# Evacuations of the output projection queued first, combinations in eight pieces, and a lead of four groups

## The chip, the cores and the metric

The kernel runs on one core of one Trainium2 chip. The metric is the device time of one execution in microseconds; less is better. The core's engines each work through a queue of their own in order: PE (matrix products), DVE (elementwise on vectors), ACT (elementwise with functions, and copies), POOL (elementwise), SP (which issues all the DMAs here). Semaphores order them between each other.

## The reference

An encoder trunk of four residual layers on 1024 tokens of width 1024, all in float32: attention (two head groups) with an output projection, an MLP, a gated unit with an output projection, another MLP, and a last norm. The part that the change touches is what follows an output projection:

```python
def _mlp(x, norm_g, w1, w2):
    h = _rmsnorm(x, norm_g)
    return x + jnp.square(jax.nn.relu(h @ w1)) @ w2
# after   x + concatenate([oa, ob]) @ w_out      (attention layer)
# and     x + y @ w_out                          (gated unit)
```

`w1` is 1024 by 4096, `w2` 4096 by 1024. The norm's factor per token is applied behind `h @ w1`, so that the products can start from `x * norm_g` before the sum of squares is known.

## The kernel before

Activations lie transposed: `x[k][:, half]` holds 128 of the 1024 features (k = 0 to 7) for 512 of the tokens (half 0 or 1). Every float32 operand of a product is split into a high half, a copy in fp32r made by ACT, and a low half, the rest, made by DVE (`hilo`, L144 to L148, `scaled`, L833); a product of two operands is three matmuls (`mm3`).

The output projection, `out_proj` (L828), goes in two column groups cg and two halves of tokens through `lin` (L272). At the end of each half four accumulators are complete, and `ev` (L869) evacuates them: DVE adds the accumulator to `x` (L872), ACT squares the sum and POOL adds the square into a running sum `ss` (L313, L314), SP stores the sum, and `combine` (L839) prepares the operands of the MLP. The MLP's first product is done with seven products of half size in place of eight (a scheme of Strassen's kind): the blocks of `x` by k < 4 or k >= 4 and half 0 or 1 are combined into seven operands `hc[i, kk]`, i = 1 to 7, kk = 0 to 3. Operands 1 and 2 are blocks alone (half 0, known early); 5 is a difference of blocks with k < 4; 7, 6, 4 and 3 need the last half of the last column group. For each of its four k, `combine` makes b22 on ACT (L850), t3 and t2 on DVE (L851, L853), and the halves of operands 7 and 6 from them; a function `rest` (L856) makes operands 4 and 3 later. The four `rest` are collected in `later`.

In `mlp` (L885) the products of the 16 groups of columns of `w1` go in the order of a table, `UP_ORDER` (L153): first i = 1 for the first `LEAD` = 3 groups, then i = 2 for these, then 7, 6, 5, 4, 3 of group 0, of group 1, of group 2, and then all seven of each further group. Product (g, i) here means group g, operand i: 12 matmuls. i = 1 fills a bank of PSUM, which ACT copies out (r1, L916); i = 2 adds onto the same bank, so it waits for that copy. i = 3 adds onto the bank of i = 5, after DVE has read it (L936). After the product (0, 7) the two `ssb` matmuls sum the squares over the features, and L321 or L324 on ACT and L325 to L331 on DVE make the norm's factor. PSUM has eight such banks, given out in turn as they come free. At each step `ahead` (L131, called at L966) makes the weights for four steps ahead (DVE adds, ACT and DVE split), and at step 1 all four `rest` run (L968 to L970).

The framework's scheduler puts the instructions of each engine into an order at build time; it is not quite the order of the text. The two passages from an output projection into an MLP are the same code, called at L881 and L1243.

Of the kernel before, what the change touches and what calls it, by code (L numbers as in the profile page):

```python
# [7 lines left out]
F32 = mybir.dt.float32  # L8
# [24 lines left out]
def tile_kernel(ctx: ExitStack, tc: tile.TileContext, I, out, upto=99, dbg=None):  # L33
# [13 lines left out]
    def nm(s):  # L47
        uid[0] += 1
        return f"{s}_{uid[0]}"

    def blk(s, dt=F32R):
        return blkp.tile([P, 2, HN], dt, tag="blk", name=nm(s))

    def tr(s, dt=F32):
        return trp.tile([P, HN], dt, tag="tr", name=nm(s))
# [10 lines left out]
    def f(ap):  # L66
        return ap.bitcast(F32)
# [30 lines left out]
    def col(i):  # L98
        return par[:, i : i + 1]
# [31 lines left out]
    def ahead(n):  # L131
        n = min(n, len(items))
        while emitted[0] < n:
            while loaded_to[0] < min(emitted[0] + LOADS, len(items)):
                items[loaded_to[0]][0]()
                loaded_to[0] += 1
            items[emitted[0]][1]()
            emitted[0] += 1
# [5 lines left out]
    def hilo(src):  # L144
        w = blk("w")
        act.copy(w[:, 0], src)  # L146
        dve.tensor_tensor(w[:, 1], src, f(w[:, 0]), op=ALU.subtract)  # L147
        return w  # L148

    LEAD = 3
    UP_ORDER = [(g, i) for i in (1, 2) for g in range(LEAD)]  # L153
    UP_ORDER += [(g, i) for g in range(16) for i in (1, 7, 2, 6, 5, 4, 3) if g >= LEAD or i not in (1, 2)]
    DOWN_ORDER = [(k, i) for pair in ((7, 1), (6, 2), (5, 4), (3,)) for k in range(16) for i in pair]
# [104 lines left out]
    def tick():  # L260
        for c in list(chains):
            if next(c, 0) == 0:
                chains.remove(c)
# [8 lines left out]
    def lin(rhs, evac, spare=1, swap=False, hook=None, run=True):  # L272


        g = gi[0]
        gi[0] += 1
        for half in range(2):
            acc = [ps("lin") for _ in range(4)]
            for k in range(KT):
                w = wt(g, k)  # L280
                r = rhs(k, half)
                for m in range(4):
                    ls = slice(m * P, (m + 1) * P)
                    if swap:
                        mm3(acc[m], r, w, ls, k == 0, k == KT - 1)
                    else:
                        mm3(acc[m], w, r, ls, k == 0, k == KT - 1)
                if run and k == 1:
                    ahead(base[g] + 4 + spare)
                if run and half == 1 and k % 2 == 1:  # L290
                    ahead(base[g] + 4 + spare + (k + 1) // 2)
                if hook is not None:
                    hook(half, k)
                tick()
            for m in range(4):
                evac(m, half, acc[m])
# [8 lines left out]
    def add_sq(k, half, xs, w_=HN):  # L305
        if (half, "n") not in sumsq:
            a = nr("ss")
            act.activation(a[:, 0:w_], xs, AF.Square)
            sumsq[half, "n"] = 1
            sumsq[half] = a  # L310
        else:
            t = tr("sq")[:, 0:w_]
            act.activation(t, xs, AF.Square)  # L313
            pool.tensor_tensor(sumsq[half][:, 0:w_], sumsq[half][:, 0:w_], t, op=ALU.add)  # L314
# [39 lines left out]
    def clear_sumsq(half):  # L354
        sumsq.pop(half)
        sumsq.pop((half, "n"))
# [455 lines left out]
    def x_tile(k):  # L812
        if k not in x:
            x[k] = blk("x", F32)
        return x[k]
# [12 lines left out]
    def out_proj(src, rhs, c, hc, hook=None):  # L828


        later, d1 = [], {}

        def scaled(i, kk, src, cc):  # L833
            t = blk("h")
            act.activation(t[:, 0], src, AF.Copy, scale=cc)
            dve.scalar_tensor_tensor(t[:, 1], src, cc, f(t[:, 0]), op0=ALU.mult, op1=ALU.subtract)
            hc[i, kk] = t

        def combine(k, half):  # L839
            kk = k % 4  # L840
            g1, n1, g2 = col(c + kk), npar[:, c + kk : c + kk + 1], col(c + 4 + kk)
            if half == 0:
                scaled(1 if k < 4 else 2, kk, x[k][:, 0], col(c + k))
            elif k < 4:
                d1[kk] = tr("d1")
                dve.tensor_tensor(d1[kk], x[k][:, 0], x[k][:, 1], op=ALU.subtract)
                scaled(5, kk, d1[kk], g1)
            else:
                b22, t3, t2 = tr("b22"), tr("t3"), d1[kk]
                act.activation(b22, x[k][:, 1], AF.Copy, scale=g2)  # L850
                dve.scalar_tensor_tensor(t3, x[kk][:, 1], n1, b22, op0=ALU.mult, op1=ALU.add)  # L851
                hc[7, kk] = hilo(t3)
                dve.scalar_tensor_tensor(t2, t2, n1, b22, op0=ALU.mult, op1=ALU.subtract)  # L853
                hc[6, kk] = hilo(t2)

                def rest():  # L856
                    dve.scalar_tensor_tensor(t2, x[k][:, 0], g2, t2, op0=ALU.mult, op1=ALU.add)
                    hc[4, kk] = hilo(t2)
                    scaled(3, kk, x[k][:, 1], g2)

                later.append(rest)

        for cg in range(2):
            for half in range(2):
                for m in range(4):
                    k = cg * 4 + m
                    sp.dma_start(x_tile(k)[:, half], src[k, :, half * HN : (half + 1) * HN])

            def ev(m, half, p_):  # L869
                k = cg * 4 + m  # L870
                xs = x[k][:, half]
                dve.tensor_tensor(xs, p_, xs, op=ALU.add)  # L872
                add_sq(k, half, xs)
                sp.dma_start(xm_dram[k, :, half * HN : (half + 1) * HN], xs)
                combine(k, half)

            lin(rhs, ev, hook=hook)
        return later

    hc = {}  # L880
    later = out_proj(I["xT"], lambda k, half: OH[k, half], C_MLP0, hc, av_rest)  # L881
    OH.clear()
    O.clear()

    def mlp(l, hc, later, c_next, last):  # L885
# [19 lines left out]
        def flush(now):  # L905
            while stores and stores[0][0] <= now:
                stores.pop(0)[1]()
# [3 lines left out]
        def up_step(g, i):  # L911
# [11 lines left out]
            if i == 7 and not r:  # L923
                for half in range(2):
                    r[half] = rstd_rows(half)
                    clear_sumsq(half)
            if i == (7 if g < LEAD else 2):
                first_u(g)
# [29 lines left out]
        def first_u(g):  # L958
            ua = banks[g, "u"] = blk("ua", F32)
            z(ua[:, 0], banks.pop((g, "x")), 0)  # L960
            store(0, g, ua[:, 0])

        pos = up_base[l]
        for n, (g, i) in enumerate(UP_ORDER):
            step[0] = n
            ahead(pos + n + 4)  # L966
            flush(n)
            if n == 1:  # L968
                while later:
                    later.pop(0)()  # L970
            up_step(g, i)
            tick()
        flush(len(UP_ORDER) + 9)
# [99 lines left out]
    def final(half, a, b, rest):  # L1073
# [13 lines left out]
        for k in range(KT):  # L1087
# [8 lines left out]
            if k % 2 == 1:  # L1096
                yield 1

    mlp(0, hc, later, C_SGU, False)
    x.clear()  # L1100
    if upto <= 3:
# [139 lines left out]
    rsq[0] = "ars"  # L1241
    hc = {}
    later = out_proj(xs_dram, lambda k, half: y[k, half], C_MLP1, hc)  # L1243
    y.clear()
    if upto <= 4:
        return dict(x=x)
    mlp(1, hc, later, None, True)
    while chains:
        tick()
# [108 lines left out]
```

## Time and profile before

| | |
|---|---|
| median of 3 runs | 2095.03 us (2094.3 to 2097.71) |
| the profiled execution | 2097.54 us, its span 2095.8 us |
| PE busy | 2036.0 us, 97% of the span |
| DVE, ACT, POOL busy | 70%, 46%, 27% |
| mean granted clock of PE | 0.992 of 2.4 GHz |

The span is from the first to the last instruction; the rest of the profiled execution's time lies around it. Times in the rows are counted from the span's start. Instructions on one engine overlap a little: the start of the next is a better measure of what one costs in a row than its own length. A releaser behind an arrow is what ended the idle time before the row's first instruction. L72 is the helper that issues every matmul.

### The profile page before, as it was taken

The page shows a single profiled execution, that of the slowest core. Times are in us where ns is not written, and L with a number is a line of the kernel's source. Part 1 is how long each engine was busy: PE and PEld are TensorE (multiplying, and loading weights), DVE is VectorE, ACT ScalarE, POOL GpSimd, SP SyncE. Part 2 cuts the span into 40 slices and gives each one's busy share as a digit, 9 for nine tenths or more (in the row PEclk, how much of TensorE's full clock was granted, in tenths as well). Part 3 has the DMA queues.
Part 4 walks back from the last instruction along what each step waited for, and adds up shares of the span by engine and source line. Part 5 has one row for each costly group of instructions (what it writes and reads, how often), then busy time and mean ns, then how long its engine had stood idle before and what let it go on. Part 6 is the DMA issues. An engine that isn't in the chain of part 4 may idle for free. (4 is left out here: it accounts for less than half of the span.)

```text
span 2095.8 us, 27079 instructions
## 1 busy us (share of the span) xinstructions
PE 2036.0 (97%) x9126; PEld 1676.2 (80%) x9126; DVE 1459.8 (70%) x2324; ACT 961.2 (46%) x1768; POOL 564.0 (27%) x437
## 2 busy tenths in 40 slices
PE   8998999999899999999999999999899999999997
PEld 7786877788688888888888888887788888888885
DVE  6878878856786666756696545556866667846975
ACT  5525677773433333435454434433433334544542
POOL 4325466543132222200002126322232223000021
PEclk9999999999999999999999999999999999999998
DMA  4364121134044444768464210432254446855542
GB/s 163 125 195 122 42 65 46 31 111 158 23 165 148 151 156 165 264 204 293 131 220 144 77 57 11 151 107 75 81 174 148 161 151 205 294 218 195 170 140 95
DMA packets 207307, 294.92 MB, mean 141 GB/s; under 512 B 19648, under 2 KB 88768, under 8 KB 207168
## 3 DMA queue, kind: packets, MB, share of 16 engines
q1 hardware_dynamic: 207168, 293.19, 42.5%
q8 instruction: 72, 1.18, 0.2%
q14 instruction: 67, 0.55, 0.1%
HBM read 207.13 MB, written 85.98 MB: 140 GB/s over the span
## 5 line engine op out<-in xcount | busy, mean ns | idle before, releaser
L72 PE MATMUL up<-h,w 128*128 128x512 f32 x1536 | 372.2, 395 | 18.6 <-ACT r L916 9.3
L72 PE MATMUL dy<-w,w 128*128 128x512 f32 x1536 | 364.7, 389 | 0.0
L72 PEld LDWEIGHTS up<-h,w 128*128 128x128 f32 x1536 | 292.9, 191 | 83.1 <-ACT r L916 10.1
L72 PEld LDWEIGHTS dy<-w,w 128*128 128x128 f32 x1536 | 288.3, 188 | 60.3 <-issue 0.5
L314 POOL TENSOR_TENSOR ss<-ss,sq 128x512 f32<-128x512 f32 x66 | 103.4, 1568 | 676.7 <-ACT sq L313 582.1
L72 PE MATMUL up<-w,w 128*128 128x512 f32 x1152 | 277.0, 390 | 0.0
L72 PE MATMUL dx<-w,w 128*128 128x512 f32 x1152 | 276.7, 389 | 0.0
L72 PEld LDWEIGHTS up<-w,w 128*128 128x128 f32 x1152 | 216.4, 188 | 46.0 <-issue 1.0
L72 PEld LDWEIGHTS dx<-w,w 128*128 128x128 f32 x1152 | 216.2, 188 | 44.9
L146 ACT CAST w<-wr 128x512 fp32r<-128x512 f32 x288 | 166.7, 620 | 136.9 <-DVE wr L179 37.3
L147 DVE TENSOR_TENSOR w<-wr,w 128x512 fp32r<-128x512 f32 x288 | 198.1, 699 | 24.2 <-ACT w L146 20.1
L72 PE MATMUL lin<-h,w 128*128 128x512 f32 x768 | 181.3, 393 | 1.1 <-POOL w L123 0.5
L72 PEld LDWEIGHTS lin<-h,w 128*128 128x128 f32 x768 | 143.3, 188 | 33.7 <-issue 2.4
L951 POOL TENSOR_TENSOR t<-ua,ub 128x512 f32<-128x512 f32 x32 | 43.9, 1371 | 459.8 <-ACT ua L898 422.9
L645 POOL TENSOR_TENSOR pp<-pe,pp 128x512 fp32r<-128x512 f32 x107 | 143.4, 1362 | 76.9 <-ACT pp L641 60.4
L147 DVE TENSOR_TENSOR w<-ur,w 128x512 fp32r<-128x512 f32 x224 | 156.0, 707 | 5.8 <-ACT w L146 5.6
L146 ACT CAST w<-ur 128x512 fp32r<-128x512 f32 x224 | 135.8, 620 | 42.3 <-DVE w L147 19.7
L147 DVE TENSOR_TENSOR w<-ws,w 128x512 fp32r<-128x512 f32 x128 | 94.0, 734 | 67.5 <-ACT w L146 67.0
L72 PE MATMUL st<-r,k 128*128 128x512 f32 (+2 forms) x384 | 131.0, 398 | 4.6 <-DVE mb L603 3.6
L146 ACT CAST w<-ws 128x512 fp32r<-128x512 f32 x128 | 79.5, 621 | 110.8 <-DVE ws L226 75.8
L898 ACT ACTIVATE ua<-ua 128x512 f32<-128x512 f32 x64 | 40.4, 633 | 179.0 <-DVE ua L897 179.0
L897 DVE SCALAR_TENSOR_TENSOR ua<-up,rstd 128x512 f32<-128x512 f32 x32 | 22.1, 690 | 139.5 <-PE up L72 139.5
(191 smaller groups left out, 3134.2 us busy)
## 6 DMA issues: line engine op xcount, KB each, us to landing
ur<-ucd SPq DMA_DIRECT2D x224, 256.0 KB, 3.6
wr<-in_w SPq DMA_DIRECT2D x256, 128.0 KB, 2.7
ucd<-t SPq DMA_DIRECT2D x128, 256.0 KB, 2.0
wr<-in_w SPq DMA_DIRECT2D x128, 256.0 KB, 3.5
ucd<-ub SPq DMA_DIRECT2D x64, 256.0 KB, 2.0
x<-in_xT SPq DMA_DIRECT2D x32, 256.0 KB, 4.6
xmd<-x SPq DMA_DIRECT2D x32, 256.0 KB, 2.1
ucd<-ua SPq DMA_DIRECT2D x32, 256.0 KB, 2.0
```

The costliest lines, as they stand in the source:

```text
L72: last_mm[0] = pe.matmul(o, l, r, start=start, stop=stop, **kw)
L146: act.copy(w[:, 0], src)
L147: dve.tensor_tensor(w[:, 1], src, f(w[:, 0]), op=ALU.subtract)
L314: pool.tensor_tensor(sumsq[half][:, 0:w_], sumsq[half][:, 0:w_], t, op=ALU.add)
L645: lo.tensor_tensor(pp[:, 1], e, f(pp[:, 0]), op=ALU.subtract)
L897: dve.scalar_tensor_tensor(dst, src, 0.0, r[half], op0=ALU.max, op1=ALU.mult)
L898: act.activation(dst, dst, AF.Square)
L951: pool.tensor_tensor(t3, ua[:, 1], ub[:, 1], op=ALU.subtract)
```

## The change

Three edits. `LEAD` goes from 3 to 4. In `out_proj` the last half of the last column group evacuates all four accumulators first, and its four combinations are put into `later`, with the four `rest` behind them. In `mlp` one piece of `later` runs per step, in the steps 0 to 7, in place of all four `rest` in step 1. The differences d1 become halves of two larger tiles instead of four small ones.

```diff
--- before.py
+++ after.py
@@ -149,7 +149,7 @@
 
 
 
-    LEAD = 3
+    LEAD = 4
     UP_ORDER = [(g, i) for i in (1, 2) for g in range(LEAD)]
     UP_ORDER += [(g, i) for g in range(16) for i in (1, 7, 2, 6, 5, 4, 3) if g >= LEAD or i not in (1, 2)]
     DOWN_ORDER = [(k, i) for pair in ((7, 1), (6, 2), (5, 4), (3,)) for k in range(16) for i in pair]
@@ -828,7 +828,7 @@
     def out_proj(src, rhs, c, hc, hook=None):
 
 
-        later, d1 = [], {}
+        later, rests, d1, pairs = [], [], {}, {}
 
         def scaled(i, kk, src, cc):
             t = blk("h")
@@ -842,7 +842,9 @@
             if half == 0:
                 scaled(1 if k < 4 else 2, kk, x[k][:, 0], col(c + k))
             elif k < 4:
-                d1[kk] = tr("d1")
+                if kk % 2 == 0:
+                    pairs[kk // 2] = blk("d1", F32)
+                d1[kk] = pairs[kk // 2][:, kk % 2]
                 dve.tensor_tensor(d1[kk], x[k][:, 0], x[k][:, 1], op=ALU.subtract)
                 scaled(5, kk, d1[kk], g1)
             else:
@@ -858,7 +860,7 @@
                     hc[4, kk] = hilo(t2)
                     scaled(3, kk, x[k][:, 1], g2)
 
-                later.append(rest)
+                rests.append(rest)
 
         for cg in range(2):
             for half in range(2):
@@ -872,10 +874,13 @@
                 dve.tensor_tensor(xs, p_, xs, op=ALU.add)
                 add_sq(k, half, xs)
                 sp.dma_start(xm_dram[k, :, half * HN : (half + 1) * HN], xs)
-                combine(k, half)
+                if cg == 1 and half == 1:
+                    later.append(lambda: combine(k, half))
+                else:
+                    combine(k, half)
 
             lin(rhs, ev, hook=hook)
-        return later
+        return later + [lambda: rests.pop(0)() for _ in range(4)]
 
     hc = {}
     later = out_proj(I["xT"], lambda k, half: OH[k, half], C_MLP0, hc, av_rest)
@@ -965,9 +970,8 @@
             step[0] = n
             ahead(pos + n + 4)
             flush(n)
-            if n == 1:
-                while later:
-                    later.pop(0)()
+            if later:
+                later.pop(0)()
             up_step(g, i)
             tick()
         flush(len(UP_ORDER) + 9)
```

On DVE at the end of the first output projection: x is a block of the stream, lin an accumulator, t3, d1 and b22 what `combine` makes, and L147 a low half. Before:

```order
L853 SCALAR_TENSOR_TENSOR d1_1246_4966<-d1_1246_4966,npar_4586,b22_1284_5268 128x512
L851 SCALAR_TENSOR_TENSOR t3_1290_5285<-x_1190_4594,npar_4586,b22_1289_5284 128x512
L853 SCALAR_TENSOR_TENSOR d1_1249_4976<-d1_1249_4976,npar_4586,b22_1289_5284 128x512
L147 TENSOR_TENSOR w_1287_5276<-d1_1246_4966,w_1287_5276 128x512
L147 TENSOR_TENSOR w_1291_5288<-t3_1290_5285,w_1291_5288 128x512
L147 TENSOR_TENSOR w_1292_5292<-d1_1249_4976,w_1292_5292 128x512
L872 TENSOR_TENSOR x_1257_4997<-lin_1273_5138,x_1257_4997 128x512
L857 SCALAR_TENSOR_TENSOR d1_1243_4956<-x_1254_4991,par_73,d1_1243_4956 128x512
L857 SCALAR_TENSOR_TENSOR d1_1246_4966<-x_1255_4993,par_73,d1_1246_4966 128x512
L857 SCALAR_TENSOR_TENSOR d1_1249_4976<-x_1256_4995,par_73,d1_1249_4976 128x512
L851 SCALAR_TENSOR_TENSOR t3_1295_5301<-x_1191_4596,npar_4586,b22_1294_5300 128x512
```

And now:

```order
L874 TENSOR_TENSOR x_1253_4994<-lin_1269_5138,x_1253_4994 128x512
L874 TENSOR_TENSOR x_1254_4996<-lin_1270_5139,x_1254_4996 128x512
L874 TENSOR_TENSOR x_1255_4998<-lin_1271_5140,x_1255_4998 128x512
L874 TENSOR_TENSOR x_1256_5000<-lin_1272_5141,x_1256_5000 128x512
L853 SCALAR_TENSOR_TENSOR t3_1283_5276<-x_1188_4590,npar_4586,b22_1282_5275 128x512
L855 SCALAR_TENSOR_TENSOR d1_1244_4961<-d1_1244_4961,npar_4586,b22_1282_5275 128x512
L147 TENSOR_TENSOR w_1284_5279<-t3_1283_5276,w_1284_5279 128x512
L147 TENSOR_TENSOR w_1285_5283<-d1_1244_4961,w_1285_5283 128x512
L853 SCALAR_TENSOR_TENSOR t3_1289_5302<-x_1189_4592,npar_4586,b22_1288_5301 128x512
L855 SCALAR_TENSOR_TENSOR d1_1244_4961<-d1_1244_4961,npar_4586,b22_1288_5301 128x512
L859 SCALAR_TENSOR_TENSOR d1_1244_4961<-x_1253_4994,par_73,d1_1244_4961 128x512
L147 TENSOR_TENSOR w_1290_5305<-t3_1289_5302,w_1290_5305 128x512
```

The fourth evacuation moved ahead of every combination, and the combinations of different k no longer run side by side; the first `rest` (L859, before L857) comes between them.

On ACT at the same place: sq is a square, r1 the copy of a lead bank, L146 a high half. Before:

```order
L313 ACTIVATE sq_1288_5280<-x_1256_4995 128x512
L850 ACTIVATE b22_1289_5284<-x_1256_4995,par_73 128x512
L146 CAST w_1287_5276<-d1_1246_4966 128x512
L146 CAST w_1291_5288<-t3_1290_5285 128x512
L146 CAST w_1292_5292<-d1_1249_4976 128x512
L313 ACTIVATE sq_1293_5296<-x_1257_4997 128x512
L850 ACTIVATE b22_1294_5300<-x_1257_4997,par_73 128x512
L916 COPY r1_1299_5324<-up_1298_5311 128x512
L916 COPY r1_1309_5367<-up_1308_5354 128x512
L146 CAST w_1296_5304<-t3_1295_5301 128x512
```

And now:

```order
L313 ACTIVATE sq_1278_5256<-x_1253_4994 128x512
L313 ACTIVATE sq_1279_5261<-x_1254_4996 128x512
L313 ACTIVATE sq_1280_5266<-x_1255_4998 128x512
L313 ACTIVATE sq_1281_5271<-x_1256_5000 128x512
L852 ACTIVATE b22_1282_5275<-x_1253_4994,par_73 128x512
L921 COPY r1_1287_5299<-up_1286_5286 128x512
L146 CAST w_1284_5279<-t3_1283_5276 128x512
L146 CAST w_1285_5283<-d1_1244_4961 128x512
L852 ACTIVATE b22_1288_5301<-x_1254_4996,par_73 128x512
L921 COPY r1_1293_5325<-up_1292_5312 128x512
L146 CAST w_1290_5305<-t3_1289_5302 128x512
```

The four squares stand together, and the first copy r1 stands behind one b22 only, where two stood behind the fourth square and all of three combinations.

## Rows read from the trace of the kernel before

**Rows 1.** Busy time by engine, the page's part 1

```profile
PE 2036.0 (97%) x9126; PEld 1676.2 (80%) x9126; DVE 1459.8 (70%) x2324; ACT 961.2 (46%) x1768; POOL 564.0 (27%) x437
```

**Rows 2.** PE's waits in the whole run: us, times, longest us

```profile
PE up L72 <- ACT r L916: 9.3, 2, 4.6
PE up L72 <- ACT w L146: 8.4, 3, 3.1
```

**Rows 3.** PE timeline, first passage: start us, us, what, count [idle before, releaser]

```profile
542.38 8.32 PE L72 MATMUL up<-h,w 128*128 128x512 f32 x36
555.33 7.07 PE L72 MATMUL up<-h,w 128*128 128x512 f32 x24 [4.63 <-ACT r L916]
565.47 4.43 PE L72 MATMUL up<-h,w 128*128 128x512 f32 x12 [3.07 <-ACT w L146]
...
572.47 1.88 PE L72 MATMUL ssb<-ss,ones 128*128 128x512 f32 x4
573.79 3.32 PE L72 MATMUL up<-w,w 128*128 128x512 f32 x12
...
583.40 2.98 PE L72 MATMUL up<-h,w 128*128 128x512 f32 x12 [0.85 <-DVE ub L936]
```

**Rows 4.** PE timeline, second passage

```profile
1449.37 8.32 PE L72 MATMUL up<-h,w 128*128 128x512 f32 x36
...
1481.25 3.32 PE L72 MATMUL up<-w,w 128*128 128x512 f32 x12
...
1492.55 4.58 PE L72 MATMUL up<-h,w 128*128 128x512 f32 x12 [2.54 <-ACT w L146]
```

**Rows 5.** Stretches: from:to, length, PE busy, granted clock, DMA share, GB/s

```profile
583.30:586.20 2.90, 2.80 (x12) 1.00 0.00 0
...
1494.60:1497.00 2.40, 2.40 (x8) 0.52 0.57 213
```

**Rows 6.** The chain that ended last: start us, us, engine, tile, count

```profile
1774.60 2.72 PE dx L72 x12
```

**Rows 7.** DVE timeline, first passage

```profile
540.54 2.05 DVE L872 TENSOR_TENSOR x<-lin,x 128x512 f32<-128x512 f32 x3 [8.36 <-PE lin L72]
542.67 1.20 DVE L851 SCALAR_TENSOR_TENSOR t<-x,npar,b 128x512 f32<-128x512 f32 x1
...
552.79 0.68 DVE L872 TENSOR_TENSOR x<-lin,x 128x512 f32<-128x512 f32 x1
...
557.06 0.74 DVE L853 SCALAR_TENSOR_TENSOR d<-d,npar,b 128x512 f32<-128x512 f32 x1
...
568.31 1.89 DVE L147 TENSOR_TENSOR w<-wr,w 128x512 fp32r<-128x512 f32 x3 [0.68 <-ACT w L146]
570.12 0.69 DVE L183 TENSOR_TENSOR wr<-wr,wr 128x512 f32<-128x512 f32 x1
574.31 0.69 DVE L325 TENSOR_SCALAR va<-ssb 128x512 f32<-128x512 f32 x1 [3.50 <-ACT y L321]
...
582.57 0.68 DVE L936 SCALAR_TENSOR_TENSOR ub<-up,u 128x512 f32<-128x512 f32 x1
...
595.67 0.69 DVE L936 SCALAR_TENSOR_TENSOR ub<-up,u 128x512 f32<-128x512 f32 x1
```

**Rows 8.** ACT timeline, first passage

```profile
554.10 0.71 ACT L850 ACTIVATE b<-x,par 128x512 f32<-128x512 f32 x1
554.71 1.05 ACT L916 COPY r<-up 128x512 f32<-128x512 f32 x2
```

**Rows 9.** POOL timeline, squares' sums in the projection's last half but one

```profile
520.27 6.41 POOL L314 TENSOR_TENSOR ss<-ss,sq 128x512 f32<-128x512 f32 x4 [13.54 <-ACT sq L313]
```

**Rows 10.** DVE timeline beside those sums

```profile
522.64 4.59 DVE L836 SCALAR_TENSOR_TENSOR h<-x,par,h 128x512 fp32r<-128x512 f32 x3
```

**Rows 11.** DVE timeline, second passage

```profile
1483.06 0.69 DVE L325 TENSOR_SCALAR va<-ssb 128x512 f32<-128x512 f32 x1 [5.26 <-ACT y L324]
...
1491.72 0.68 DVE L936 SCALAR_TENSOR_TENSOR ub<-up,u 128x512 f32<-128x512 f32 x1
```

## The prediction

> **What bounds the kernel now.** I read the busy shares first: PE works 97% of the span [rows 1], so only what makes PE wait, or run slowly, moves the end. The view of waits over the whole run then names the two largest of PE's waits: the copy r1 of a bank (L916) and casts of L146, 9.3 and 8.4 us in five pieces [rows 2]. The timeline of PE puts them, but for the second passage's last (below), in the two passages from an output projection into an MLP. In the first, PE starts the products at 542.38, three of them without a break, and then stands still for 4.63 us, later 3.07 and 0.85 [rows 3]. A product of 12 matmuls takes 2.72 us where nothing disturbs it [rows 6], the two matmuls of ssb 573.79 - 572.47 = 1.32 [rows 3]. From 542.38 to the start of product (0, 3) at 583.40 there are ten products and ssb: 10 x 2.72 + 1.32 = 28.52 us of work in 41.02, so 12.50 are lost. In the second passage the same stretch goes from 1449.37 to 1492.55 [rows 4]: 43.18, of which 14.66 are lost. More than the waits is lost since TensorE's clock falls after a long one: behind the 0.85 us the granted clock was 1.00 (2.4 GHz), behind the 2.54 us in the second passage it was 0.52 in a stretch of 2.4 us, nearly all of it at 1.2 GHz [rows 5]. The product behind that wait took 4.58 us in its row, the one behind 0.85 us 2.98 [rows 3, 4]: 1.60 more.
>
> Why PE waits is read from DVE and ACT. Three of the four last evacuations (L872) run at 540.54, the fourth only at 552.79, behind the combinations of the first three [rows 7]. ACT's queue holds that evacuation's square and b22 ahead of the copy r1, which thus comes at 554.71 [rows 8]; product (0, 2) adds onto that bank and waits for the copy. The third wait, before (0, 3), is another chain: from ssb through L325 to L936 on DVE, which must have read the bank of (0, 5). In the second passage the row before (0, 3) names a cast of ACT; L936 ended at 1492.40 there, and as in the first passage PE started 0.15 us later [rows 3, 4, 7, 11], so I take L936 for it.
>
> **Part by part: the late evacuation.** The four evacuations are now in a row, so no copy r1 sits behind a combination except by one b22 each. The copy of bank 0 follows the first b22 at about 545.2, and (0, 2) needs it only after four products, at 542.38 + 4 x 2.72 = 553.26. The 4.63 us go in both passages. What is late next? I walked DVE's new order. The fourth evacuation starts at 540.54 + 2.05 = 542.59; before, from its start to the end of b22 it took 554.10 + 0.71 - 552.79 = 2.02 us [rows 7, 8], so DVE's first combination starts at about 544.65, after 1.4 us of idling that is new.
>
> **The combinations and the weights.** From there to L183, the last before L325, DVE has 37 instructions; before there were 36 of the same kinds, from 542.67 to 570.12 + 0.69 = 570.81, that is 28.14 us [rows 7]. Two waits of 0.68 us for casts are in it (one is in the row at 568.31), and the toll of four adds on POOL: while four adds ran from 520.27 for 6.41 us, 1.60 each [rows 9], three DVE instructions took 4.59 us, 1.53 each [rows 10], against 0.74 for an L853 of the same form at 557.06, with POOL idle [rows 7]: a toll of 0.79 per add. (28.14 - 1.36 - 4 x 0.79) / 36 = 0.656 us each. After the change the four adds run together from about 542, where the square of the first evacuation ends as before, for 6.4 us; 3.75 us of that, 2.3 adds, lie beside DVE's work: 544.65 + 37 x 0.656 + 2.3 x 0.79 = 570.8. Between, PE asks for weights: (3, 2) starts at 542.38 + 7 x 2.72 = 561.42 and its low half is DVE's 22nd instruction, done at about 560.9; that is tight, (2, 2) has 1.7 us to spare. A miss there costs nothing of its own as long as DVE's end sets the next wait.
>
> [...]
>
> **The wait before (0, 3).** Now 12 products and ssb lie ahead of it: 542.38 + 33.96, plus 0.44 since the product after ssb took 3.32 instead of 2.88 in its row [rows 3], is 576.8. ssb would end at 542.38 + 9 x 2.72 + 1.32 = 568.2, before DVE is through at 570.8, so L325 starts at 570.8. From L325 to the end of L936 it took 582.57 + 0.68 - 574.31 = 8.94 us [rows 7], with the same instructions in the same order as now, and PE went on 0.15 later: (0, 3) starts at 579.9. Against 583.40 + 2 x 2.72 for the two products that are now done earlier, 588.84, that is 8.98 us gained. But PE waits 3.1 us there instead of 0.85, and I charge the 1.60 us of a slow product: 7.4. With four groups, four banks of x, (0, 7), two of ssb and (0, 6) fill all eight, so (0, 5) takes the bank that L325 frees; L325 ends at 571.5 and PE could have it at 571.3: no cost of its own.
>
> **Second passage.** The same, 906.99 us later: DVE is through at 1477.8. ssb would end at 1475.2, and L325 followed its end by 1.81 before (1481.25 to 1483.06, a table load on ACT is in it) [rows 4, 11], so 1477.0: DVE is the later one. L325 to the end of L936 took 9.34 [rows 11]: (0, 3) at 1487.25, against 1492.55 + 5.44: 10.7 gained, with a slow product in both.
>
> **Nothing or little.** d1 as halves of larger tiles, and eight pieces instead of one: no instruction more. Groups 1 to 3 have five products each, 13.6 us of PE; DVE took 595.67 - 582.57 = 13.1 for such a group [rows 7], so PE stays the later one. On SP the eight loads, 128 KB each, of a fourth group's pair of w1 tiles move from between the first stores of results into the projection's last column group, and DVE does that group's first two additions before the passage: both lie beside the projection's last half, where DVE idles 8.36 us ahead of the evacuations [rows 7]. Without that cover they would cost DVE two instructions, 1.3 us.
>
> Sum: 7.4 + 10.7 = 18.1 us. The profiled execution took 2097.54, so 2079.4; it lies 2.5 above the median of 2095.03, so I predict 2077.
>
> **Bounds.** Best: DVE ahead of ssb in both passages; L325 then starts at 568.7 (0.52 after ssb, 573.79 to 574.31) and 1477.0, and short waits spare both slow products: 11.0 + 11.5 + 1.6 = 24.1, 2071. Worst: every instruction as dear as the mean of before with waits and tolls in it, 28.14 / 36 = 0.78: DVE is through 2.8 us later, 4.6 + 7.9 = 12.5, 2082.5.
>
> **Rivals.** (A) DVE is no limit, as in the best bound: 2071. For it: ACT's casts mostly have an instruction's time of lead. Against it: 37 instructions in 24 us without a gap leave none. (B) Hand-overs between ACT and DVE: 23 of the 37 take a high half that ACT has just made. Two waits of 0.68 us were in the old stretch; five more per passage cost 2 x 3.4: 2084. (C) Slower: the same mechanism in full. If all 23 waited 0.68 us, DVE would be through 15.6 us later and (0, 3) would start 6.7 and 4.9 us after what it had, with 1.6 for the clock: 2108. It decides from 13 late hand-overs per passage in the first (8.98 / 0.68). For it: combinations and casts now alternate piece by piece, with r1 copies and b22 between. Against it: in the new order nearly each cast has another DVE instruction between its source and its low half. (D) The gain is given back in groups 1 to 3, DVE having only 0.5 us to spare in 13.6: 2095. Against it: in the old trace PE has no wait after 583.40 although such groups followed.
>
> **Chances.** Forecast 0.55, its own range 2072 to 2082.5; A 0.12, B 0.18, C 0.07, D 0.08. Faster by over 0.2%, which is about 4.2 us and what a measurement of this kernel can tell from no change: 0.85; within: 0.08; slower: 0.07. From 2070 to 2086 all but C, D and some tails are held.
>
> **What would show it.** Right: no wait of PE for r1, four evacuations back to back on DVE, the copy of bank 0 near 545; PE's one long wait in each passage before (0, 3), at some 580 and 1487, for DVE. Wrong: waits before (2, 2) or (3, 2) for a low half, DVE rows with many idle gaps of 0.7 released by ACT (B, C), or waits of PE in groups 1 to 3 (D).

## The result, and the profile after

The changed kernel takes 2077.49 us (median of 5 runs, 2075.91 to 2078.3) against 2095.03 us before: a ratio of 0.9909, 95% interval 0.9895 to 0.9924. It is faster, and the predicted 2077 is met. The profiled execution took 2075.91 us, its span 2074.1.

Busy shares of the profiled execution, as [rows 1]:

```profile
PE 2028.4 (98%) x9126; PEld 1672.3 (81%) x9126; DVE 1456.5 (70%) x2324; ACT 962.2 (46%) x1768; POOL 563.8 (27%) x437
```

PE's waits of the whole run in the products of the MLPs (us in total, times, longest), as [rows 2]:

```profile
PE up L72 <- ACT w L146: 3.0, 1, 3.0
PE up L72 <- DVE ub L941: 2.3, 1, 2.3
```

Before, the second passage had two waits more, beside the 2.54 us of [rows 4]:

```profile
1462.33 7.35 PE L72 MATMUL up<-h,w 128*128 128x512 f32 x24 [4.63 <-ACT r L916]
1472.47 4.88 PE L72 MATMUL up<-h,w 128*128 128x512 f32 x12 [2.79 <-ACT w L146]
```

Six pieces of waiting in the two passages (the five of [rows 2] and the 0.85 us for L936), 18.5 us in total, have become two of 5.4 us, and none is for a copy r1. PE's timeline in the first passage, as [rows 3]:

```profile
542.89 21.92 PE L72 MATMUL up<-h,w 128*128 128x512 f32 x96
564.65 2.89 PE L72 MATMUL up<-w,w 128*128 128x512 f32 x12
567.37 1.88 PE L72 MATMUL ssb<-ss,ones 128*128 128x512 f32 x4
...
574.57 2.88 PE L72 MATMUL up<-w,w 128*128 128x512 f32 x12
579.80 2.97 PE L72 MATMUL up<-h,w 128*128 128x512 f32 x12 [2.35 <-DVE ub L941]
```

And in the second, as [rows 4]:

```profile
1440.28 21.92 PE L72 MATMUL up<-h,w 128*128 128x512 f32 x96
...
1477.99 2.97 PE L72 MATMUL up<-h,w 128*128 128x512 f32 x12 [3.03 <-ACT w L146]
```

All eight products of the lead (96 matmuls) now run without a break. The only wait is the one before (0, 3). In the second passage its row names a cast of ACT. But the read of (0, 5)'s bank, L941 on DVE (rows below), ended at 1477.84 and PE started 0.15 later, as it started 0.14 after L941 in the first passage, where the same cast began only at 580.29, after PE had started. So I take L941 for both. From the first product to the start of (0, 3) there are 12 products and ssb, 33.96 us of work, in 36.91 and 37.71 us: 2.95 and 3.75 lost where 12.50 and 14.66 were.

DVE in the first passage, as [rows 7]:

```profile
541.05 2.73 DVE L874 TENSOR_TENSOR x<-lin,x 128x512 f32<-128x512 f32 x4 [6.60 <-PE lin L72]
545.22 0.75 DVE L853 SCALAR_TENSOR_TENSOR t<-x,npar,b 128x512 f32<-128x512 f32 x1 [1.44 <-POOL ss L314]
545.89 1.79 DVE L855 SCALAR_TENSOR_TENSOR d<-d,npar,b 128x512 f32<-128x512 f32 x1
547.60 1.78 DVE L147 TENSOR_TENSOR w<-t,w 128x512 fp32r<-128x512 f32 x1
549.30 0.68 DVE L147 TENSOR_TENSOR w<-d,w 128x512 fp32r<-128x512 f32 x1
...
560.69 0.67 DVE L147 TENSOR_TENSOR w<-wr,w 128x512 fp32r<-128x512 f32 x1
...
570.13 0.68 DVE L183 TENSOR_TENSOR wr<-wr,wr 128x512 f32<-128x512 f32 x1
570.73 0.68 DVE L325 TENSOR_SCALAR va<-ssb 128x512 f32<-128x512 f32 x1
...
578.98 0.68 DVE L941 SCALAR_TENSOR_TENSOR ub<-up,u 128x512 f32<-128x512 f32 x1
```

ACT and POOL there, as [rows 8, 9]:

```profile
544.41 0.71 ACT L852 ACTIVATE b<-x,par 128x512 f32<-128x512 f32 x1
545.86 0.59 ACT L921 COPY r<-up 128x512 f32<-128x512 f32 x1 [0.74 <-PE up L72]
```

```profile
542.54 6.29 POOL L314 TENSOR_TENSOR ss<-ss,sq 128x512 f32<-128x512 f32 x4 [15.35 <-ACT sq L313]
```

The evacuations stand in a row; the first copy r1 comes at 545.86, waiting for PE alone. The first combination (545.22) waits 1.44 us; its row names POOL, but ACT's b22, which it reads, ended at 545.12. From 545.22 to L325 no DVE row names an idle gap, and L325 follows L183 directly. Two instructions beside POOL's adds cost 1.7 us each, and everything from 549.30 on runs at 0.6 to 0.7. In the second passage L325 has one short wait, for ACT (DVE's rows first, as [rows 11], then ACT's):

```profile
1467.53 0.68 DVE L183 TENSOR_TENSOR wr<-wr,wr 128x512 f32<-128x512 f32 x1
1468.49 0.69 DVE L325 TENSOR_SCALAR va<-ssb 128x512 f32<-128x512 f32 x1 [0.29 <-ACT y L324]
...
1477.16 0.68 DVE L941 SCALAR_TENSOR_TENSOR ub<-up,u 128x512 f32<-128x512 f32 x1
```

```profile
1466.47 1.28 ACT L324 ACT_TABLE_LOAD   x1
```

The granted clock behind the first wait, as [rows 5]:

```profile
579.50:582.00 2.50, 2.20 (x10) 1.00 0.00 0
```

It is 1.00: no slow product. So it is behind the second (1.00 from 1477.90 to 1481.00, the product 2.97 us in its row).

Where the time came from: the first products begin at 542.89 instead of 542.38 (0.5 lost before the passages); from there to the second passage's first product it is 897.39 us instead of 906.99 (9.6 gained); from that to the end 633.8 instead of 646.4 (12.6 gained). That is the whole difference of the spans, 21.7.

### The profile page after: what moved, and what is told of

It is laid out like the page before. It is cut to its first block, busy times and chain, and to the rows that moved or that the text cites. A ratio compares the mean times of both kernels' runs of the same rounds, so it can differ in the third digit from the quotient of the medians.

```text
span 2074.1 us, 27073 instructions
## 1 busy us (share of the span) xinstructions
PE 2028.4 (98%) x9126; PEld 1672.3 (81%) x9126; DVE 1456.5 (70%) x2324; ACT 962.2 (46%) x1768; POOL 563.8 (27%) x437
## 4 chain that ended last, share of the span: by engine, by line
PE 85%; DVE 9%; issue 2%; ACT 2%; POOL 1%; DMA 1%; SPq 0%; DVEq 0%; POOLq 0%; ACTq 0%
PE up L72 26%; PE lin L72 17%; PE dy L72 17%; PE dx L72 13%; PE av L72 4%; PE st L72 3%; PE mx L72 1%; PE vp L72 1%; DVE w L147 1%; PE kp L72 1%; DVE mb L603 1%; DVE rec L691 1%; PE bc L72 1%; DVE pp L643 1%; PE hss L72 1%
## 5 line engine op out<-in xcount | busy, mean ns | idle before, releaser
L72 PE MATMUL up<-h,w 128*128 128x512 f32 x1536 | 363.1, 389 | 5.4 <-ACT w L146 3.0
L72 PEld LDWEIGHTS up<-h,w 128*128 128x128 f32 x1536 | 288.1, 188 | 66.1 <-ACT w L146 3.4
L146 ACT CAST w<-wr 128x512 fp32r<-128x512 f32 x288 | 167.5, 621 | 144.7 <-DVE wr L179 39.0
L147 DVE TENSOR_TENSOR w<-wr,w 128x512 fp32r<-128x512 f32 x288 | 201.6, 709 | 23.9 <-ACT w L146 19.9
L147 DVE TENSOR_TENSOR w<-ur,w 128x512 fp32r<-128x512 f32 x224 | 155.9, 706 | 6.6 <-ACT w L146 6.4
L146 ACT CAST w<-ur 128x512 fp32r<-128x512 f32 x224 | 135.9, 620 | 43.1 <-DVE w L147 20.5
L147 DVE TENSOR_TENSOR w<-ws,w 128x512 fp32r<-128x512 f32 x128 | 93.9, 734 | 68.6 <-ACT w L146 68.1
L146 ACT CAST w<-ws 128x512 fp32r<-128x512 f32 x128 | 79.5, 621 | 112.0 <-DVE ws L226 75.8
L72 PE MATMUL av<-pp,v 128*128 128x512 f32 x384 | 109.2, 395 | 3.5 <-DVE pp L643 1.6
```

The costliest lines, as they stand in the source:

```text
L72: last_mm[0] = pe.matmul(o, l, r, start=start, stop=stop, **kw)
```

## The experiments

My theory (T): the three edits are links of one chain, DVE's queue. Evacuating first frees the copies r1, the pieces let the weights of the second operands through on DVE, and the longer lead covers what is left; each alone leaves the next wait standing. Rivals: the lead is what counts (L), or the order of the evacuations is (E). All kernels keep d1 as halves of larger tiles. The table has every run. The ratio is to runs of the kernel before taken beside each kernel (their medians go from 2095.03 to 2097.15), so it is not the quotient of the medians shown. "From the first product" is the profiled span less the start of the first passage's first product; it leaves out the stages ahead, in which executions of one and the same kernel differ by up to 3 us (the lead of five starts its passage at 539.53 in one profile and 542.60 in another).

| kernel | timed median, us | ratio to before, 95% interval | from the first product, us |
|---|---|---|---|
| before | 2095.03 | | 1553.4 |
| changed | 2077.49 | 0.9909 (0.9895 to 0.9924) | 1531.2 |
| changed, again | 2077.45 | 0.9911 (0.9898 to 0.9925) | 1534.3 |
| changed, third profile | 2077.32 (one run) | | 1532.9 |
| lead 4 alone | 2095.71 | 0.9998 (0.9989 to 1.0008) | 1554.8 |
| lead 3 | 2086.35 | 0.9950 (0.9937 to 0.9962) | 1543.0 |
| pieces bunched | 2095.42 | 0.9995 (0.9987 to 1.0004) | 1552.5 |
| evacuations not first | 2089.30 | 0.9968 (0.9956 to 0.9981) | 1544.5 |
| lead 5 | 2070.34 | 0.9877 (0.9863 to 0.9890) | 1527.3 |
| lead 5, again | 2071.48 | 0.9879 (0.9864 to 0.9894) | 1527.3 |
| norm's chain late | 2072.61 | 0.9890 (0.9875 to 0.9905) | 1530.1 |
| four more on DVE | 2085.09 | 0.9945 (0.9933 to 0.9958) | 1541.0 |
| lead 5, chain late | 2068.50 | 0.9866 (0.9850 to 0.9882) | 1527.1 |
| lead 5, chain late, again | 2071.24 | 0.9878 (0.9861 to 0.9894) | 1527.1 |

**The lead alone.** From the changed kernel:

```diff
-                if cg == 1 and half == 1:
-                    later.append(lambda: combine(k, half))
-                else:
-                    combine(k, half)
+                combine(k, half)
...
-        return later + [lambda: rests.pop(0)() for _ in range(4)]
+        return rests
...
-            if later:
-                later.pop(0)()
+            if n == 1:
+                while later:
+                    later.pop(0)()
```

> The lead of four groups alone: evacuations and combinations as before, all four rests at step 1 (d1 as halves of larger tiles in this and all following kernels). Theory T (each edit takes away the wait that the next one would leave: the lead gives cover, the evacuations free the r1 copies, the pieces let the weights of (1, 2) to (3, 2) through on DVE): the copy of bank 0 still ends near 555.3 and PE waits some 2 us before (0, 2), where 4.63 stood. Then the low half of (1, 2) is the 31st of DVE's instructions after 542.67, behind all rests: at 0.74 to 0.78 us each near 565.5, so PE waits some 7 us before (1, 2). (0, 3) then comes near 587, 7 us later than in the changed kernel's first passage; with slow products behind the waits 2090 to 2095. Rival L (two more products of cover are what the change is worth): 2077 to 2082, no wait over 4 us. Rival E (only the order of the evacuations matters): 2095, with PE's wait for r1 still at 4.6.

PE's timeline of that kernel, first passage:

```profile
555.53 3.01 PE L72 MATMUL up<-h,w 128*128 128x512 f32 x12 [1.93 <-ACT r L918]
565.67 11.13 PE L72 MATMUL up<-h,w 128*128 128x512 f32 x36 [7.13 <-ACT w L146]
...
590.24 3.01 PE L72 MATMUL up<-h,w 128*128 128x512 f32 x12 [0.79 <-DVE ub L938]
```

The two waits are 1.93 and 7.13, as T has them; nothing is gained, and L falls. E's 2095 fits the total, but not the wait for r1, which E left at 4.6. The total came out 0.7 above T's range: (0, 3) starts 3 us later than I had put it, since the chain behind ssb has a wait of its own (0.79) and behind the 7.13 the matmuls run slowly (36 of them in 11.13 us instead of 8.3).

**The lead of three**, everything else as changed:

```diff
-    LEAD = 4
+    LEAD = 3
```

> The changed kernel with a lead of three groups: evacuations first and pieces between the products. Theory T (DVE's chain up to the read of (0, 5)'s bank sets (0, 3), whatever the lead): that read is the 49th of DVE's instructions from the first combination at 545.2; at 0.607 us each and 2.1 us of toll beside POOL it ends near 577, (0, 3) starts near 577.3, where PE would be due at 571.9. The wait grows from 2.35 to some 5 us, and against the changed kernel (two products more done by 579.8) each passage loses 2.9 us: 2083 to 2086 with the clock. Rival L (the cover of two products counts in full): 5.44 lost per passage, 2088 to 2091. Rival E (the order of the evacuations alone matters): within 1 us of the changed kernel, 2077.

PE's timeline of it, first passage:

```profile
571.71 0.73 PE L72 MATMUL up<-w,w 128*128 128x512 f32 x2 [3.34 <-DVE w L147]
574.77 5.30 PE L72 MATMUL up<-h,w 128*128 128x512 f32 x12 [2.33 <-DVE ub L941]
```

PE waits 5.67 us in two pieces, the first inside (0, 4) for the last rest's low half, both for DVE. 2086.35 lies 0.3 above T's range and below L's: two products less of cover cost 4.4 us a passage with the clock, not their full 5.44 and not nothing. The stretch from the first product to (0, 3) tells T from L without the clock behind it: 35.07 and 35.19 us (second passage: 1443.10 to 1478.29) with two products fewer in it, that is 3.6 and 2.9 lost against the changed kernel, where T had 2.9 and L 5.44.

**The pieces bunched.** All combinations at step 0, all rests at step 1:

```diff
-            if later:
-                later.pop(0)()
+            for _ in range((4, 4)[n] if n < 2 else 0):
+                later.pop(0)()
```

> The changed kernel with its eight pieces bunched: the four combinations at step 0, the four rests at step 1. Theory T: no wait for r1 before (0, 2) over 1 us, but the low half of (1, 2) is again behind all rests on DVE, the 30th instruction after 545.2: near 565. PE is through with (0, 2) at 556.5 and waits 8 us before (1, 2), (0, 3) near 586.7, 6.9 later than in the changed kernel; with slow products behind the waits 2090 to 2095. Rival E (the evacuations in a row carry the gain): 2077 to 2080. Rival L (the lead carries it): 2077 to 2082.

PE's timeline, first passage:

```profile
551.20 3.02 PE L72 MATMUL up<-h,w 128*128 128x512 f32 x12 [0.47 <-ACT r L921]
560.98 1.22 PE L72 MATMUL up<-h,w 128*128 128x512 f32 x2 [6.76 <-ACT w L146]
```

PE's first passage starts at 539.68 here. The wait for r1 is nearly gone, and all of the gain with it: 6.76 us for the weights of (1, 2), which stand behind the rests. E and L fall here; T's range is missed by 0.4 us.

**The evacuations not first**, lead four and one rest per step:

```diff
-                if cg == 1 and half == 1:
-                    later.append(lambda: combine(k, half))
-                else:
-                    combine(k, half)
+                combine(k, half)
...
-        return later + [lambda: rests.pop(0)() for _ in range(4)]
+        return rests
```

> The changed kernel without the evacuations first: each of the last four evacuations is followed by its combination, as before, the rests run one per step from step 0, lead four. Theory T: the copy of bank 0 ends near 555.3 as before, PE waits 2 us before (0, 2); the low half of (1, 2) is the 25th DVE instruction after 542.67, near 561, another 3 us; (3, 2) just in time near 566.5; ssb ends near 573.3 and (0, 3) starts near 583, 3.1 later than in the changed kernel: 2083 to 2087. Rival L: 2077 to 2080, since lead and pieces carry it and the 2 us before (0, 2) only shorten the wait before (0, 3). Rival E: 2093 to 2095.

PE's timeline, first passage:

```profile
555.71 3.04 PE L72 MATMUL up<-h,w 128*128 128x512 f32 x12 [1.92 <-ACT r L918]
561.66 11.61 PE L72 MATMUL up<-h,w 128*128 128x512 f32 x36 [2.92 <-ACT w L146]
```

Both waits as expected (2 and 3); the total 2.3 above T's range, with the product behind the 2.92 slow (36 matmuls in 11.61 instead of 8.3) and 0.79 more before (0, 3).

So each edit, taken out, opens the next wait in the queue. That each alone leaves the next wait standing is shown for the lead only: the evacuations alone and the pieces alone were not run. The larger tiles for d1 are in all of these kernels, and with the lead alone they gained nothing. What of the rest? The next kernels take the wait before (0, 3), with the changed kernel beside them:

> The changed kernel once more, beside the next three on the same chip: 2077.5 by its first timing (2075.9 to 2078.3), and again one wait in each passage, before (0, 3), of 2.4 and 3.0 us. The clock behind these two waits is open: 1.00 in the first profile of this kernel.

**Four more instructions on DVE**, in the last rest:

```diff
+                    for _ in range(4 if kk == 3 else 0):
+                        dve.tensor_tensor(t2, t2, t2, op=ALU.max)
                     hc[4, kk] = hilo(t2)
```

> The changed kernel with four more DVE instructions (a maximum of d1 with itself) in the last rest, ahead of L325 and of the read of (0, 5)'s bank. Theory T (DVE's queue sets (0, 3)): each costs its 0.6 to 0.75 us in each passage, the waits grow from 2.4 and 3.0 to 4.8 to 5.4 and 5.4 to 6: 2082 to 2084 at full clock, up to 3.2 more if the products behind the waits run slowly. Rival S (PE waits for the chain behind ssb, DVE having room ahead of it): 2077 to 2079. On the clock: if the length of a wait alone decides, the products behind these two run slowly (4.5 us and more instead of 2.98); if what counts is whether PE had stood still before in the same passage, they don't.

PE's timeline, both passages:

```profile
582.46 4.59 PE L72 MATMUL up<-h,w 128*128 128x512 f32 x12 [3.60 <-ACT w L146]
...
1484.69 5.46 PE L72 MATMUL up<-h,w 128*128 128x512 f32 x12 [4.33 <-ACT w L146]
```

DVE's read of (0, 5)'s bank in both (L943 in this kernel):

```profile
581.63 0.68 DVE L943 SCALAR_TENSOR_TENSOR ub<-up,u 128x512 f32<-128x512 f32 x1
...
1483.87 0.68 DVE L943 SCALAR_TENSOR_TENSOR ub<-up,u 128x512 f32<-128x512 f32 x1
```

With two short stops ahead (0.24 and 0.92; 0.24 and 0.40) PE waits 4.76 and 4.97 us, 2.4 and 2.0 more than without the four; the second is below T's 5.4 to 6. From the first product (542.55 and 1444.59) to (0, 3) it is 39.91 and 40.10 us, 3.0 and 2.4 more than in the changed kernel. From the first combination up to and with that read DVE has 56 instructions in both passages, where the changed kernel has 51 and 52 (the scheduler moved one, L179, ahead of the read in the first passage): five and four more at 0.6 us each. PE's rows name a cast, but (0, 3) starts 0.15 and 0.14 us after L943's end. DVE's queue sets (0, 3), and S falls. The products behind ran slowly, and 2085.09 lies within what that allows. On the clock the run is inconclusive, since the dose also put the short stops ahead.

**The lead of five**, everything else as changed:

```diff
-    LEAD = 4
+    LEAD = 5
```

> The changed kernel with a lead of five groups. Theory T (what is left is the chain from ssb to the read of (0, 5)'s bank): two products more lie ahead of ssb, so DVE's combinations are done before it (41 instructions from 545.2, at 572.2) and L325 follows ssb, which ends near 574.1. But five banks of the lead, (0, 7) and two of ssb fill all eight, so (0, 6) waits for L325: 0.9 us in the first passage, some 2.5 in the second, where a table load stands ahead on ACT. The read of (0, 5)'s bank ends 8.9 us after L325 starts, near 583.2, with PE due at 583.4: PE loses 1.1 and 2.8 us in the passages where it lost 2.95 and 3.75: 2074 to 2076. Rival B (banks decide: with none free the first products of each group wait too): 2079 or more. Rival C (the lead is pure cover, both waits go): 2071.

PE's rows, first passage, and DVE's:

```profile
571.99 3.08 PE L72 MATMUL up<-w,w 128*128 128x512 f32 x12 [0.65 <-DVE va L325]
...
580.40 2.92 PE L72 MATMUL up<-h,w 128*128 128x512 f32 x12
```

```profile
568.11 0.69 DVE L183 TENSOR_TENSOR wr<-wr,wr 128x512 f32<-128x512 f32 x1
571.24 0.69 DVE L325 TENSOR_SCALAR va<-ssb 128x512 f32<-128x512 f32 x1 [2.44 <-ACT y L321]
```

ACT's and PE's rows, second passage:

```profile
1463.01 1.28 ACT L324 ACT_TABLE_LOAD   x1
1466.37 0.69 ACT L324 ACTIVATE y<-ssb,eps 128x512 f32<-128x512 f32 x1 [2.08 <-PE ssb L72]
```

```profile
1467.83 3.00 PE L72 MATMUL up<-w,w 128*128 128x512 f32 x12 [0.64 <-DVE va L325]
```

DVE now idles ahead of L325, PE has one short wait for the bank that L325 frees, and none before (0, 3). 2070.34 is 3.7 us below T's range: I had put 2.5 us on the second passage's bank for the table load on ACT, but with the longer lead ACT loads it before ssb ends, and the wait is 0.64 there too. And with no long wait left, no product runs slowly (2.92 to 3.08 us in the rows above). The four times are 2068.62, 2068.69, 2072.0 and 2072.01, so the median lies between two pairs; from the first product the kernel takes 3.9 us less than the changed one's shortest, where T's waits had 2.8. My "C" came nearest; the chain of L325 is as T has it, its price was not.

**The norm's chain late.** The two ssb matmuls, L325 to L331 and the first result of group 0 behind the read of (0, 5)'s bank:

```diff
-            if i == 7 and not r:
-                for half in range(2):
-                    r[half] = rstd_rows(half)
-                    clear_sumsq(half)
-            if i == (7 if g < LEAD else 2):
+            if i == 2 and g >= LEAD:
+                first_u(g)
+            if i == 7 and 0 < g < LEAD:
                 first_u(g)
...
                 dve.scalar_tensor_tensor(ub[:, 1], banks[g, 5], -1.0, sums[g][1], op0=ALU.mult, op1=ALU.subtract)
+                if not r:
+                    for half in range(2):
+                        r[half] = rstd_rows(half)
+                        clear_sumsq(half)
+                    first_u(0)
```

> The changed kernel with the two ssb matmuls and the norm's chain (L325 to L331, and the first result of group 0) put behind the read of (0, 5)'s bank instead of behind (0, 7). Theory T (PE waits before (0, 3) since DVE works through the norm's chain first): the read is now the 7th instruction behind L183 on DVE, done near 575, and PE is due at 577.3: no wait in either passage, 2.5 and 3.3 us gained: 2071 to 2073. DVE's deferred work fits into groups 1 to 3: the next such read, of (1, 5), would be done near 590 with PE due at 590.9. Rival D (DVE's debt of nine instructions, 5.5 us, is paid in groups 1 to 3): the waits come back before (1, 3) or (2, 3), 2076 to 2078. Rival Z (the wait before (0, 3) comes from the sums of (0, 6) and (0, 7), which are not moved): 2077.

PE's row with the longest wait, first passage (the view ends inside the product):

```profile
604.52 0.70 PE L72 MATMUL up<-h,w 128*128 128x512 f32 x2 [1.89 <-DVE ub L939]
```

The median is within T's range, but the trace gives half of that to D: the wait before (0, 3) is gone, and 1.89 us stand before (2, 3), with 0.30 and 0.82 in the second passage. DVE's deferred instructions are paid two groups later. From the first product it is 1530.1, only 1.1 below the changed kernel's shortest; the rest of the 4.8 us between the medians I put down to the missing slow products and to the stages ahead (its passage started at 540.18), a split that was not measured.

**Both**: lead five and the late chain, beside the lead of five again.

> The lead of five groups once more, as the mark for the next kernel on the same chip: 2070.3 by its first timing, with one wait for a bank of 0.65 us in each passage and none before (0, 3).

> Lead of five and the norm's chain behind the read of (0, 5)'s bank, together. Theory T (with five groups only the wait for the bank that L325 frees is left, 0.65 us and a slower product behind it in each passage; with ssb later (0, 6) and (0, 5) need no bank of it): PE loses about 0.5 us per passage in place of 1.47, 2068 to 2069. Rival D (DVE's debt comes back in groups 1 to 4, as the 1.89 us before (2, 3) with four groups): 2070 to 2072, no better than the lead alone.

PE's only row with a wait in the first passage:

```profile
577.54 2.99 PE L72 MATMUL up<-w,w 128*128 128x512 f32 x12 [0.65 <-DVE va L325]
```

T was wrong here: the same 0.65 for the bank of L325 stands before (0, 4), where it stood before (0, 6). From the first product the two kernels take the same. Its median was lower all the same (2068.50 against 2071.48), so it ran once more:

> The lead of five with the late norm's chain once more. From the start of the first passage to the end it took as long as the lead of five alone (1527.1 and 1527.3 us), so the 2 to 3 us between their medians should lie ahead of the first passage, where the products begin at 539.5 in some executions and at 542.6 in others of one and the same kernel. If that is chance, single times between 2068 and 2072 come here too, and the median may be as high as 2071; if the kernel itself begins the passage earlier, all times are again within 2068.4 to 2068.7.

Single times between 2068.36 and 2071.83, median 2071.24: chance, in the stages ahead of the passages. In the two profiles of the lead of five PE's wait for an operand of the first stage (L360) ends at 37.57 and at 38.99 us, and its wait at the first output projection (L301) at 472.08 and 475.14, so the 3 us are there before any code that the edits touch; what brings them was not sought. The lead of five, with or without the late chain, is the best version: 0.9866 to 0.9879 of before, and from the first product 4 to 7 us below the changed kernel.

**The clock**, in a third profile of the changed kernel:

> The changed kernel's profile a third time, for the clock behind its two waits. In the first profile both products behind them ran at 1.00 (2.97 us each), in the second both slowly (4.39 and 4.54) after waits of the same length. If the clock depends on where the execution happens to stand, either may come, and the span follows: 2074 with none slow, about 2075.5 with one, 2077 with two.

PE's rows behind the two waits, in the second profile and in the third, and a stretch of the second:

```profile
579.69 4.39 PE L72 MATMUL up<-h,w 128*128 128x512 f32 x12 [2.37 <-DVE ub L941]
...
1479.32 4.54 PE L72 MATMUL up<-h,w 128*128 128x512 f32 x12 [3.01 <-ACT w L146]
```

```profile
579.53 2.98 PE L72 MATMUL up<-h,w 128*128 128x512 f32 x12 [2.35 <-DVE ub L941]
...
1477.75 4.24 PE L72 MATMUL up<-h,w 128*128 128x512 f32 x12 [3.03 <-ACT w L146]
```

```profile
579.50:582.00 2.50, 2.31 (x6) 0.50 0.00 0
```

The same program, the same waits to 0.02 us: none, two and one slow product, and spans of 2074.1, 2077.1 and 2075.5, some 1.5 us for each (from (0, 3) to the start of the product after the next two it is 8.25 us at full clock, and 9.67, 9.87 and 9.89 with the slow ones).

## Why the prediction was right

**The waits for r1** went, by the step given: the copy ended at 546.45 and (0, 2) was due at 542.89 + 4 x 2.72 = 553.8. **DVE's walk** held: 37 instructions from 545.22 to 570.81, 25.6 us (26.1 predicted), with 1.44 us of new idling ahead of them (1.4 predicted). Its two parts were a little off, against each other: the toll of POOL's adds was 2 x (1.705 - 0.634) = 2.1 us, not 1.8, the other 35 instructions 0.634 each, not 0.656. By 2.3 adds that is 0.93 each, where 0.79 was charged. L325 started at 570.73 (570.8 predicted; these times agree better than the lengths do, since the passage itself began 0.51 later than before), no low half came late, and that of (3, 2), done at 561.36, was 0.6 us early for PE's 561.93. **The chain from L325** to the end of L941 took 8.93 us (8.94 predicted), and (0, 3) started at 579.80 (579.9), 36.91 us after the first product (37.5). In the second passage the stretch was 37.71 us (37.88). There the prediction had DVE through 0.8 us after ACT's result behind the table load; the order came out the other way, and L325 waited 0.29 for ACT. That DVE's queue sets (0, 3) is shown by the four added instructions, 0.6 us each, and by the lead of three.

**The step that was mis-sized is the clock.** I charged 1.60 us for a slow product in the first passage and left one standing in the second, as if a wait of 3 us always brought it. The price held (1.4 to 1.6 us each), the certainty did not: three profiles of the changed kernel have three slow products behind six such waits. From the first product the gain was 22.2, 19.1 and 20.5 us where the sum had 18.1; 19.1, with both products slow, is the like-for-like number, 1.0 off, of which 0.8 lies in the two stretches up to (0, 3), both shorter than predicted. That the median fits to 0.5 us owes something to the offset of 2.5 that I took for the execution profiled before: a slow product more or less in that one execution, or the start of the passage, may be part of it, which was not measured. To that extent the 0.5 is luck.

**Rivals.** A fell: a wait stands before (0, 3), with DVE busy until L325 in the first passage and until 0.29 us before it in the second. B and C fell: DVE had one wait ahead of the first combination and none for a cast between the 37 instructions. D did not happen here, PE having no wait in groups 1 to 3; but its mechanism is real, since the kernel with the late chain paid 1.89 us before (2, 3).

## What to carry to other kernels

When several producers share one queue, walk that queue in its new order and write down when each consumer asks; an edit that frees one item moves the wait to the next, and here the longer lead gained nothing alone or with the evacuations first, 0.3% with the pieces, and 0.9% with both. Cover on the consumer's side paid here only where the queue delivered everything else in time: a lead of four instead of three was worth 0 us with the old queue and 9 us with the new. The price per wait for the clock was an average here, not a constant (three slow products, 1.4 to 1.6 us each, behind six waits); judge it from several profiles of one program.

## What the runs showed of the hardware

The profile gives the granted clock as a share of full speed; no run here shows what that is in GHz. Behind one and the same wait of 2.35 to 2.37 us it was 1.00 in two executions and 0.50 in a third; behind 3.01 to 3.03 us the product took 2.97, 4.54 and 4.24 us. Across the kernels a product was slow behind 2.04 us (lead four alone, second passage: 4.58 us) and at full clock behind 2.04 us (evacuations not first, second passage: 2.99 us):

```profile
1499.58 4.58 PE L72 MATMUL up<-h,w 128*128 128x512 f32 x12 [2.04 <-ACT w L146]
```

```profile
1490.86 2.99 PE L72 MATMUL up<-h,w 128*128 128x512 f32 x12 [2.04 <-ACT w L146]
```

The waits of 0.64 to 0.92 us in PE's rows above were followed by full clock (products of 2.98 to 3.08 us), and so were the five of 1.89 to 1.93 us in the kernels with the lead alone, with the evacuations not first and with the late chain (products of 3.01 to 3.04 us). Nor does the clock always fall at the wait. In the second profile it was 0.50 right behind the first wait (above). Behind the second wait of the third profile the first six of the product's twelve matmuls took 1.68 us and the other six 2.56, where in the first profile, at 1.00, they took 1.61 and 1.36: that product began at nearly the pace of full clock and slowed down while PE worked. What PE had done ahead in the passage doesn't sort them, since in the changed kernel it ran 34 us without a break ahead of both outcomes. What decides it in a given execution was not tried.
